# Attention in a hybrid encoder layer: the values product for four query blocks at once, with y_b parts, operand places and y_a low parts moved

## The chip, the cores and the metric

One core of a Trainium2 chip. TensorE (PE) multiplies and transposes into PSUM, VectorE (DVE), ScalarE (ACT) and GpSimd (POOL) do the elementwise work, SyncE (SP) issues most DMAs. The metric is the device time of one execution in microseconds.

## What is computed

One layer with sandwich norms, sequence 1024, width 1024, eight heads of 64, float32. Cut to what matters here:

```python
h = rms_norm(x, norm_mix_pre)
q, k, v, u, gates = split(h @ w_in)
# 64-row chunks; chunk c's queries see the keys of chunks c-8 .. c
y_a = chunk_band_attention(q, k, v, rel_bias) @ w_attn_out
y_b = multiscale_pool(u, w_pool_group, pool_scale) @ w_pool_out
g_a, g_b = split(sigmoid(gates + b_gate))
mix = (g_a * y_a + g_b * y_b) @ w_o
x = x + rms_norm(mix, norm_mix_post)
x = x + rms_norm(conv_gated_ffn(rms_norm(x, norm_ffn_pre), ...), norm_ffn_post)
```

## The kernel before

Each float32 operand is split into a high part (rounded to the matmul's type, by ACT) and a low part (the rest, a subtraction on DVE or POOL); a product is up to three matmuls: high x high, high x low, low x high. The helper `split` (L78) records both halves of a split and `mm3` (L84) the three products, so many instructions have these two lines: tiles tell them apart.

The stages in order: the input projection (tiles X_i, Y_i, Z_i), the attention with the y_b projection woven in, the y_a projection (tiles y), the product with w_o (tiles wops, L1117), and the feed-forward part (X_u, Y_u, Z_u and later X, Y, Z).

**Attention.** A head h has four steps J, each of two query blocks a of 128 rows. `scores(h, J)` multiplies queries and keys into `pst` (L850 for blocks with all 640 keys, L859 for the earlier, shorter ones); DVE adds the bias and takes the maximum (`sm`, L866), ACT takes the exponential (`pe`, L868), DVE the reciprocal (L870), POOL scales `pe` (L872). `transposed(J, pes)` turns `pe` block by block (L893, tiles `tp`, up to four in a PSUM bank); `split` copies each bank to `pth` (ACT) and `ptl` (DVE). There are two such pairs of buffers, for even and for odd J, each with six slots of 256 columns: a slot is a block of 128 keys, its columns are the two query blocks, and the corners that lie outside the band are zeroed once by POOL. `values_of(h, J)` multiplies the values `vv` with each slot, high and low, into `f` (L918): 256 columns at a time, 2, 4, 6 and 6 slots for J = 0 to 3. After every second J, ACT and DVE add the two halves of `f` (`sm2`, L926, L927) and split the sum into `ath` and `atl`, the left operand of y_a.

**y_b.** `yb_units` is a generator of 32 parts, six matmuls each (`ybp`, 128x512). The table `NU` says how many parts stand in each iteration i of the loop over the 32 (h, J) steps.

**Order.** Iteration i writes the scores of step i, the transposes of step i-1, y_b parts and the values of step i-2. A scheduler then sets the order of each engine's instructions from the written order and priorities; on the chip each engine runs its queue in that order and waits on semaphores.

**y_a.** Eight blocks m of 24 matmuls `y` (128x512, L84). `out_block` splits the weights `wr_ya`: the low part `wl_ya` on DVE for m = 0 and on POOL for the others. DVE then multiplies by the gate (L1036), adds y_b's part (L1037) and splits into `mix`. Two of the four pieces of w_o are split there too (`woh` on ACT, `wol` on POOL), the other two behind it on DVE. `y` has two PSUM buffers of two banks.

Of the kernel before, what the change touches and what calls it, by code (L numbers as in the profile page):

```python
# [17 lines left out]
P = 128  # L18
# [27 lines left out]
def trunk(ctx, tc, xn, xt, w_first, w_in, cols, gain_pre, bias, w_ao, w_pg, w_po, w_o, gains, w_up, w_dn, out):  # L46
# [25 lines left out]
    ident = const.tile([P, P], F32, name="ident")  # L72
# [293 lines left out]
    with ExitStack() as ph:  # L366
# [73 lines left out]
        A.activation(warm, warm, AF.Sqrt)  # L440
        make_identity(nc, ident)
# [338 lines left out]
    edge = ap_.tile([P, 8], F32, name="edge")  # L780
    G.memset(edge, 0.0)
# [28 lines left out]
    with ExitStack() as ph:  # L810
# [8 lines left out]
        psf.tile([P, 512], F32, tag="f", name="bankf")  # L819

# [17 lines left out]
        def scores(h, J):  # L838
# [3 lines left out]
            for a in range(2):  # L842
# [4 lines left out]
                if n == 640:  # L847
                    for c in range(2):
                        for x, kk in enumerate((kh, kl)):
                            last["pst"] = nc.tensor.matmul(  # L850
                                pst[:, 512 * c:512 * c + 320], qs[:, j * P:(j + 1) * P],
                                kk[:, k0 + 320 * c:k0 + 320 * c + 320],
                                start=x == 0, stop=x == 1)
                    sv = pst.rearrange("p (c n) -> p c n", c=2)[:, :, :320]
                    bv = bt.rearrange("p (c n) -> p c n", c=2)
# [8 lines left out]
                so = sm.rearrange("p (c n) -> p c n", c=2) if n == 640 else sm[:, :n]  # L864
# [11 lines left out]
        def transposed(J, pes):  # L876

            pth, ptl = PT[J % 2]
            fl = [t.rearrange("p s q -> p (s q)") for t in (pth, ptl)]
            (pa, na), (pb, nb) = pes  # L880
            sa, sb = 5 - na, 6 - nb
            if J == 0:
                banks = [[(pa, 0, 1, sa, 0), (pb, 0, 2, sb, 1)]]
            elif J == 1:
                banks = [[(pa, 0, 3, sa, 0)], [(pb, 0, 4, sb, 1)]]
            else:
                banks = [[(pa, 1, 4, 1, 0)], [(pa, 0, 1, 0, 0), (pb, 0, 1, 1, 1)], [(pb, 1, 4, 2, 1)]]
            for runs in banks:
                tp = psT.tile([P, 512], F32, tag="t", name="tp")
                c = 0  # L890
                for pe, b0, n, s0, a in runs:
                    for b in range(b0, b0 + n):
                        nc.tensor.transpose(tp[:, c * P:(c + 1) * P], pe[:, b * P:(b + 1) * P], ident)  # L893
                        c += 1
                if J >= 2 and len(runs) == 2:
                    moves = [(0, 2, [t[:, 0:768].rearrange("p (b q) -> p b q", b=2)[:, :, :P] for t in fl])]
                else:
                    moves, c = [], 0
                    for pe, b0, n, s0, a in runs:
                        moves.append((c, n, [t[:, s0:s0 + n, a * P:(a + 1) * P] for t in (pth, ptl)]))  # L900
                        c += n
                for c, n, (hi, lo) in moves:
# [659 lines left out]
```

## Time and profile before

| | |
|---|---|
| median of 3 runs | 1236.28 us (1236.08 to 1236.38) |
| the profiled execution | 1236.29 us; span 1234.5 us |
| PE, DVE, ACT, POOL busy | 1224.8, 949.9, 667.7, 211.5 us |
| attention with y_b | about 321.7 to 453.9 us |
| y_a | about 453.9 to 503.1 us |
| granted clock | 0.998 |

Times in the rows are microseconds from the start of the span, or ns where said. In a timeline row stand the start, the length, the engine, the line, the operation, out<-in, the shape and how many rows were merged; in brackets the engine's idle time before it and what ended that. In a row of windows stand the window, its length, each engine's busy time with the number of instructions, then the clock, the DMA share and GB/s. A matmul's length includes its passage through the array, which overlaps the next one's, so the distance between starts is what a matmul costs.

### The profile page before, as it was taken

Reading aid. Unit: us, or ns where it says so; the run is one execution under the profiler, and the core shown is the slowest. Engines: PE = TensorE matmul, PEld = TensorE weight load, DVE = VectorE, ACT = ScalarE, POOL = GpSimd, SP = SyncE. Lnnn points to the kernel's source line nnn. Section 1 sums busy time; section 2 is a strip of 40 time slices with the busy share of each in tenths; the row PEclk is TensorE's granted clock in tenths of the full one; section 3 lists DMA queues with packets and bytes.
Section 4 is the critical chain, followed back from the end, with each engine's and each line's share of the span. In section 5 each row is a group of like instructions: output and inputs, shape, how many; then the busy total and the mean of one; then the engine's idle time right before and its main releaser. Section 6 shows DMA issues by size and latency. Waiting matters only on the chain.

```text
span 1234.5 us, 16243 instructions
## 1 busy us (share of the span) xinstructions
PE 1224.8 (99%) x5743; PEld 1020.3 (83%) x5743; DVE 949.9 (77%) x1551; ACT 667.7 (54%) x1171; POOL 211.5 (17%) x184
## 2 busy tenths in 40 slices
PE   9999999999999999999999999999999999999997
PEld 7888888888889987888888888888888888888886
DVE  5898677866788878756799887667666675999968
ACT  6764355555577773434546555554545455445553
POOL 0000000043254545000000112433333300000000
PEclk9999999999999999999999999999999999999999
DMA  9879245438886845322352332122122117902103
GB/s 329 332 261 347 85 148 206 155 123 263 294 273 214 264 175 210 137 86 78 110 198 109 111 145 103 70 84 102 52 102 86 60 68 255 350 18 103 35 1 137
DMA packets 63857, 193.84 MB, mean 157 GB/s; under 512 B 6048, under 2 KB 6688, under 8 KB 58656
## 3 DMA queue, kind: packets, MB, share of 16 engines
q1 hardware_dynamic: 55712, 176.55, 40.6%
q10 hardware_dynamic: 7056, 12.59, 2.7%
q0 software_dynamic: 1008, 3.67, 0.7%
q8 instruction: 45, 0.74, 0.2%
q14 instruction: 36, 0.29, 0.1%
HBM read 139.84 MB, written 52.95 MB: 156 GB/s over the span
## 4 chain that ended last, share of the span: by engine, by line
PE 92%; DVE 6%; issue 1%; DMA 0%; ACT 0%; POOL 0%; DVEq 0%; SPq 0%; ACTq 0%
PE X_u L84 19%; PE X_i L84 12%; PE Y_u L84 10%; PE Y_i L84 9%; PE X L84 7%; PE wops L1117 7%; PE Z_u L84 4%; PE y L84 4%; PE Y L84 4%; PE ybp L84 3%; PE f L918 3%; PE tp L893 2%; PE Z_i L84 2%; PE first L466 2%; PE pst L850 1%; DVE a L1407 1%
## 5 line engine op out<-in xcount | busy, mean ns | idle before, releaser
L1241 DVE SCALAR_TENSOR_TENSOR hc<-hu,cv,hc 128x1022 f32<-128x1022 f32 (+1 forms) x88 | 115.5, 1315 | 27.8 <-ACT hc L1236 27.8
L78 ACT CAST wh_u<-s_u 128x512 fp32r<-128x512 f32 x88 | 54.5, 619 | 90.1 <-PE Y_u L84 47.7
L78 DVE TENSOR_TENSOR wl_u<-s_u,wh_u 128x512 fp32r<-128x512 f32 x88 | 62.4, 712 | 33.9 <-ACT wh_u L78 33.9
L78 ACT CAST wh_i<-s_i 128x512 fp32r<-128x512 f32 x64 | 39.9, 623 | 77.8 <-PE X_i L84 36.5
L78 ACT CAST wh_u<-wup 128x512 fp32r<-128x512 f32 x60 | 37.3, 622 | 51.7 <-PE X_u L84 27.5
L78 DVE TENSOR_TENSOR wl_i<-s_i,wh_i 128x512 fp32r<-128x512 f32 x64 | 46.5, 727 | 21.2 <-ACT wh_i L78 16.1
L1236 ACT ACTIVATE hc<-hu,cv 128x1024 f32<-128x1024 f32 x44 | 54.7, 1245 | 9.8 <-DVE hu L1185 8.9
L202 POOL TENSOR_TENSOR s_i<-win 128x512 f32<-128x512 f32 x4 | 5.9, 1480 | 257.0 <-DVE wl_i L78 246.5
L202 POOL TENSOR_TENSOR s_u<-wup 128x512 f32<-128x512 f32 x15 | 25.7, 1713 | 139.4 <-DVE wl_u L78 139.4
L78 DVE TENSOR_TENSOR ptl<-tp,pth 128x512 fp32r<-128x512 f32 (+3 forms) x80 | 42.9, 552 | 7.7 <-ACT pth L78 7.1
L868 ACT ACTIVATE pe<-sm,st 128x640 f32<-128x640 f32 (+2 forms) x64 | 44.4, 695 | 7.6 <-DVE st L866 7.5
L872 POOL TENSOR_SCALAR pe<-pe,st 128x640 f32<-128x640 f32 (+4 forms) x58 | 40.8, 708 | 43.5 <-DVE st L870 29.3
L78 ACT CAST pth<-tp 128x512 fp32r<-128x512 f32 (+3 forms) x80 | 36.4, 475 | 15.9 <-PE tp L893 11.0
L78 DVE TENSOR_TENSOR wl_u<-wup,wh_u 128x512 fp32r<-128x512 f32 x60 | 43.0, 719 | 1.2 <-ACT wh_u L78 0.5
L1246 ACT ACTIVATE hc<-hc 128x1024 f32<-128x1024 f32 x22 | 23.4, 1063 | 37.0 <-DVE hc L1241 36.9
L84 PE MATMUL ybp<-mx,wh_yb 128*128 128x512 f32 x128 | 43.3, 412 | 0.0
L866 DVE CUSTOM_DVE_ANT_0 sm<-pst,bt 128x640 f32<-128x640 f32 (+2 forms) x64 | 40.7, 652 | 2.9 <-issue 1.7
L206 POOL TENSOR_TENSOR s_u<-s_u,wup 128x512 f32<-128x512 f32 x15 | 19.4, 1292 | 102.2 <-DVE wl_u L78 99.6
L918 PE MATMUL f<-pth,vv 128*128 128x256 f32 x144 | 36.5, 286 | 0.0
L918 PE MATMUL f<-ptl,vv 128*128 128x256 f32 x144 | 36.5, 287 | 0.0
L208 POOL TENSOR_TENSOR s_u<-wup 128x512 f32<-128x512 f32 x15 | 32.2, 2143 | 23.5 <-DVE wl_u L78 23.5
L893 PE MATMUL tp<-ident,pe 128*128 128x128 f32 x240 | 35.4, 275 | 0.2
(524 smaller groups left out, 4136.2 us busy)
## 6 DMA issues: line engine op xcount, KB each, us to landing
wup<-in_w_up SPq DMA_DIRECT2D x22, 1024.0 KB, 5.0
win<-in_w_in SPq DMA_DIRECT2D x16, 1024.0 KB, 7.2
g_d<-hc SPq DMA_DIRECT2D x20, 512.0 KB, 2.6
sig_d<-d ACTq DMA_DIRECT2D x32, 256.0 KB, 2.1
a<-g_d SPq DMA_DIRECT2D x8, 1024.0 KB, 11.5
b<-in_w_dn SPq DMA_DIRECT2D x8, 1024.0 KB, 12.7
w<-in_w_in SPq DMA_DIRECT2D x12, 512.0 KB, 7.3
x<-in_xn SPq DMA_DIRECT2D x8, 512.0 KB, 8.9
```

What stands on the lines that cost most here:

```text
L78: return A.copy(hi, src), (eng or V).tensor_tensor(lo, src, hi.bitcast(F32), ALU.subtract)
L84: nc.tensor.matmul(ps, a[i], b[i], start=start and i == 0 and p == 0, stop=stop and i == n - 1 and p == 2, skip_group_check=True,)
L202: self.eng.tensor_tensor(self.s1, self.w21, self.w22, ALU.add)
L208: self.eng.tensor_tensor(self.s3, self.w11, self.w21, ALU.subtract)
L866: V.tensor_tensor_reduce(so, sv, bv, -1.0, 3e38, ALU.add, ALU.min, st[:, 0:1])
L868: A.activation(pe[:, :n], sm[:, :n], AF.Exp, scale=-1.0, bias=st[:, 0:1], accum_out=st[:, 1:2])
L872: (V if 4 * h + J in (0, 1, 31) else G).tensor_scalar(pe[:, :n], pe[:, :n], st[:, 2:3], 1.0, ALU.mult, ALU.mult)
L893: nc.tensor.transpose(tp[:, c * P:(c + 1) * P], pe[:, b * P:(b + 1) * P], ident)
L918: nc.tensor.matmul(fo, vv[:, kb, e].rearrange("p a d -> p (a d)"), t[:, s], start=s == slots[0] and x == 0, stop=s == slots[-1] and x == 1)
L1117: nc.tensor.matmul(ps[:, 512 * c:512 * c + 512], a[k // 4][:, k % 4, sl], wo[k][b][:, 512 * c:512 * c + 512], start=k == 0 and x == 0, sto ...
L1236: A.activation(c, hu, AF.Identity, scale=cv[:, C_CW + 88 + b:C_CW + 89 + b], bias=cv[:, C_CB + b:C_CB + b + 1])
L1241: V.scalar_tensor_tensor(c[:, n:], hu[:, :S - n], cv[:, w:w + 1], c[:, n:], ALU.mult, ALU.add)
```

## The change

1. Values. One pair of buffers of 20 blocks of 128 columns takes the place of the two pairs: five key blocks for each of four query blocks, so that the place of query block a and key offset d is 5a + d. `values_of` runs only after odd J, for four query blocks: for each key block one product over just the query blocks that see it, a strided operand of 1 to 4 blocks (128 to 512 columns). For J = 1 these are 4, 3, 2 and 1 blocks, for J = 3 they are 4, 4, 3, 3, 2, 2, 1 and 1; each high and low. No zeroed corners are left.
2. Order. In an iteration the y_b parts now stand right after the scores, then the values of the last pair, then the transposes. `NU` gives two parts in every even iteration from i = 4 and none in odd ones.
3. Scores of a 640-key block go as 384 + 256 columns in one row of `pst`, not as two of 320 in two banks.
4. Places. `edge` grows from 8 to 360 columns, `edge2` of 80 columns is new, and `ident` is made later. None is read but `ident`: they move what lies behind them. In the built programs the first bytes of the operands, modulo 512 bytes, are: ath 448 before and 64 now, pth/ptl 256 and 64, ident 480 and 64, pe 256 and 64; vv, wh_ya and the keys' high part are at 64 in both.
5. y_a. The low parts of all weights `wr_ya`, and of the two w_o pieces that are split in this stage, are made by DVE.

```diff
-    edge = ap_.tile([P, 8], F32, name="edge")
-    G.memset(edge, 0.0)
+    ap_.tile([P, 360], F32, name="edge")
...
+        atn.tile([P, 80], F32, name="edge2", bufs=1)
...
-                    for c in range(2):
+                    for c in (slice(0, 384), slice(384, 640)):
                         for x, kk in enumerate((kh, kl)):
                             last["pst"] = nc.tensor.matmul(
-                                pst[:, 512 * c:512 * c + 320], qs[:, j * P:(j + 1) * P],
-                                kk[:, k0 + 320 * c:k0 + 320 * c + 320],
+                                pst[:, P + c.start:P + c.stop], qs[:, j * P:(j + 1) * P],
+                                kk[:, k0 + c.start:k0 + c.stop],
                                 start=x == 0, stop=x == 1)
...
-                banks = [[(pa, 1, 4, 1, 0)], [(pa, 0, 1, 0, 0), (pb, 0, 1, 1, 1)], [(pb, 1, 4, 2, 1)]]
+                banks = [[(pa, 0, 4, k, 0)], [(pa, 4, 1, k, 4), (pb, 0, 1, k + 1, 0)], [(pb, 1, 4, k + 1, 1)]]
...
-            fo = f[:, 256 * (J % 2):256 * (J % 2) + 256]
-            for s in slots:
-                kb = 2 * J - 4 + s
-                for x, t in enumerate(PT[J % 2]):
-                    nc.tensor.matmul(fo, vv[:, kb, e].rearrange("p a d -> p (a d)"),
-                                     t[:, s], start=s == slots[0] and x == 0,
-                                     stop=s == slots[-1] and x == 1)
             if J % 2 == 0:
                 return
+            grid = [t.rearrange("p (a d) q -> p a d q", a=4) for t in PT]
+            slots = (4, 5, 6, 7) if J == 1 else (3, 4, 2, 5, 1, 6, 0, 7)
+            for s in slots:
+                kb = 2 * J - 6 + s
+                a0, a1 = max(0, s - 4), min(3, s)
+                for x, t in enumerate(grid):
+                    flat = t.rearrange("p a d q -> p (a d) q")
+                    at = 5 * a0 + s - a0
+                    nc.tensor.matmul(f[:, a0 * P:(a1 + 1) * P], vv[:, kb, e].rearrange("p a d -> p (a d)"),
+                                     flat[:, at:at + 4 * (a1 - a0) + 1:4],
+                                     start=s == slots[0] and x == 0, stop=s == slots[-1] and x == 1,
+                                     skip_group_check=True)
...
-        NU = [2, 2, 0, 1, 0, 1, 1, 2] + [0, 1, 1, 2] * 5 + [0, 1, 1, 1, 1, 1]
+        PT = [atn.tile([P, 20, P], F32R, name=f"pt{x}", bufs=1) for x in "hl"]
+        NU = [2, 2, 1, 1] + [2, 0, 2, 0] * 5 + [2, 0, 1, 0] + [1, 0, 1, 0, 1, 0]
...
+            with tc.issue_after(last["pst"].ins) if i < 2 else nullcontext():
+                for _ in range(NU[i]):
+                    next(units)
+            if i >= 2 and steps[i - 2][1] % 2:
+                values_of(*steps[i - 2])
             if 1 <= i <= len(steps):
                 transposed(steps[i - 1][1], pend.pop(i - 1))
...
-            out_block(wr, m, ath, atl, lambda s: y[:, s], "ya", G if m else V)
+            out_block(wr, m, ath, atl, lambda s: y[:, s], "ya", V)
...
-                split_wo(wraw[m // 2 - 1], wopa, G)
+                split_wo(wraw[m // 2 - 1], wopa)
```

What the scheduler makes of it is seen in the engines' queues. First PE in the middle of the attention, where a head's last transposes (J = 3) and the values that need them stand. Before:

```order
L859 MATMUL pst_3760<-qk3_3448 128x512
L859 MATMUL pst_3760<-kl3_3449,qk3_3448 128x512
L84 MATMUL ybp_3668<-mx09_2114,wh_yb3_3664 128x512
L893 MATMUL tp_3730<-ident_77,pe_3629 128x128 x4
L893 MATMUL tp_3770<-ident_77,pe_3704 128x128
L893 MATMUL tp_3770<-ident_77,pe_3714 128x128 x2
L84 MATMUL ybp_3668<-mx19_2115,wh_yb3_3664 128x512
L84 MATMUL ybp_3668<-mx09_2114,wl_yb3_3665 128x512
L84 MATMUL ybp_3668<-mx09_2114,wh_yb3_3664 128x512
L84 MATMUL ybp_3668<-mx19_2115,wh_yb3_3664 128x512
L84 MATMUL ybp_3668<-mx09_2114,wl_yb3_3665 128x512
L918 MATMUL f_3737<-pth1_3036,vv1_3214 128x256
```

The four transposes of bank tp_3730 are the last that the twelve products f_3737 need. Now, at the same place of a later head:

```order
L83 MATMUL ybp_4031<-mx05_1595,wh_yb5_4027 128x512
L916 MATMUL f_3973<-pth_3030,vv1_3207 128x512
L83 MATMUL ybp_4031<-mx15_1596,wh_yb5_4027 128x512
L891 MATMUL tp_3946<-ident_159,pe_3850 128x128 x4
L916 MATMUL f_3973<-ptl_3031,vv1_3207 128x512
L891 MATMUL tp_3995<-ident_159,pe_3901 128x128
L891 MATMUL tp_3995<-ident_159,pe_3911 128x128 x2
L850 MATMUL pst_4003<-qk4_3657 128x384
L916 MATMUL f_3973<-pth_3030,vv1_3207 128x512
L850 MATMUL pst_4003<-kl4_3658,qk4_3657 128x384
L850 MATMUL pst_4003<-qk4_3657 128x256
L850 MATMUL pst_4003<-kl4_3658,qk4_3657 128x256
```

The last transposes are now tp_3946; the third f (key block 4, high) needs them through ACT, the fourth, behind the score products that follow, through DVE. Five y_b products between transposes and values have become one f, three transposes and a score product.

PE again, where the values of J = 1 stand, now (before, they stood a step later, with y_b parts in between):

```order
L891 MATMUL tp_4051<-ident_159,pe_3969 128x128 x4
L850 MATMUL pst_4058<-qk4_3657 128x384
L850 MATMUL pst_4058<-kl4_3658,qk4_3657 128x384
L850 MATMUL pst_4058<-qk4_3657 128x256
L850 MATMUL pst_4058<-kl4_3658,qk4_3657 128x256
L850 MATMUL pst_4070<-qk4_3657 128x384
L850 MATMUL pst_4070<-kl4_3658,qk4_3657 128x384
L850 MATMUL pst_4070<-qk4_3657 128x256
L850 MATMUL pst_4070<-kl4_3658,qk4_3657 128x256
L916 MATMUL f_4082<-pth_3030,vv2_3665 128x512
L891 MATMUL tp_4096<-ident_159,pe_4011 128x128
L916 MATMUL f_4082<-ptl_3031,vv2_3665 128x512
```

Between the last transposes (tp_4051) and the first low product stand eight score products, one f and one transpose.

DVE in the y_a stage, blocks m = 2 and 3, before:

```order
L1036 TENSOR_TENSOR ya_4949<-y,ya_4949 128x1024
L1037 TENSOR_TENSOR ya_4949<-ya_4949 128x1024
L78 TENSOR_TENSOR mix00l<-ya_4949,mix00h 128x512
L78 TENSOR_TENSOR mix10l<-ya_4949,mix10h 128x512
L1036 TENSOR_TENSOR ya_4989<-y,ya_4989 128x1024
L1037 TENSOR_TENSOR ya_4989<-ya_4989 128x1024
L78 TENSOR_TENSOR mix00l<-ya_4989,mix00h 128x512
L78 TENSOR_TENSOR mix10l<-ya_4989,mix10h 128x512
```

and now:

```order
L1018 TENSOR_TENSOR ya_4843<-y,ya_4843 128x1024
L77 TENSOR_TENSOR wl_ya_5022<-wr_ya_4928,wh_ya_5021 128x512
L1019 TENSOR_TENSOR ya_4843<-ya_4843 128x1024
L77 TENSOR_TENSOR wol<-wo_4978,woh 128x1024
L77 TENSOR_TENSOR mix00l<-ya_4843,mix00h 128x512
L77 TENSOR_TENSOR mix10l<-ya_4843,mix10h 128x512
L1018 TENSOR_TENSOR ya_4883<-y,ya_4883 128x1024
L77 TENSOR_TENSOR wol<-wo_4978,woh 128x1024
L1019 TENSOR_TENSOR ya_4883<-ya_4883 128x1024
L77 TENSOR_TENSOR wl_ya_5072<-wr_ya_4976,wh_ya_5071 128x512
L77 TENSOR_TENSOR wl_ya_5107<-wr_ya_5018,wh_ya_5106 128x512
```

The low parts wl_ya and wol, which stood on POOL, are now between DVE's own instructions of the block.

More of the change, by code (lines that the diff above doesn't have):

```diff
@@ L440, in trunk @@
         A.activation(warm, warm, AF.Sqrt)
+        ident = const.tile([P, P], F32, name="ident")
         make_identity(nc, ident)
@@ L890, in transposed @@
                 c = 0
-                for pe, b0, n, s0, a in runs:
+                for pe, b0, n, a, d in runs:
                     for b in range(b0, b0 + n):
@@ L894, in transposed @@
                         c += 1
+                c = 0
                 if J >= 2 and len(runs) == 2:
[L896 to L902, printed above, removed]
-                    split(hi, lo, tp[:, c * P:(c + n) * P].rearrange("p (b q) -> p b q", b=n))
@@ L905, in trunk @@
[L905 removed]
+                    runs = [(None, 4, 2, k, 4)]
+                for pe, b0, n, a, d in runs:
+                    at = 5 * a + d
+                    split(PT[0][:, at:at + n], PT[1][:, at:at + n],
+                          tp[:, c * P:(c + n) * P].rearrange("p (b q) -> p b q", b=n))
+                    c += n
         def values_of(h, J):
             m, e = h // 2, h % 2
[L909 to L920 removed]
@@ L958, in trunk @@
         load_wy(2)
-        PT = []
-        for i in range(2):
-            pth = atn.tile([P, 6, 256], F32R, name=f"pth{i}", bufs=1)
-            ptl = atn.tile([P, 6, 256], F32R, name=f"ptl{i}", bufs=1)
-            for t in (pth, ptl):
-                G.memset(t[:, 0, 128:256].bitcast(F32), 0.0)
-                G.memset(t[:, 5, 0:128].bitcast(F32), 0.0)
-            PT.append((pth, ptl))
+        PT = [atn.tile([P, 20, P], F32R, name=f"pt{x}", bufs=1) for x in "hl"]
         units = yb_units()
-        NU = [2, 2, 0, 1, 0, 1, 1, 2] + [0, 1, 1, 2] * 5 + [0, 1, 1, 1, 1, 1]
+        NU = [2, 2, 1, 1] + [2, 0, 2, 0] * 5 + [2, 0, 1, 0] + [1, 0, 1, 0, 1, 0]
         steps = [(h, J) for h in range(H) for J in range(4)]
@@ L978, in trunk @@
                 pend[i] = scores(h, J)
-            if i == 1:
-                with tc.issue_after(last["pst"].ins):
-                    for _ in range(NU[i]):
-                        next(units)
+            with tc.issue_after(last["pst"].ins) if i < 2 else nullcontext():
[3 more added lines that the diff above has]
+                values_of(*steps[i - 2])
             if 1 <= i <= len(steps):
                 transposed(steps[i - 1][1], pend.pop(i - 1))
-            if i == 0:
-                with tc.issue_after(last["pst"].ins):
-                    for _ in range(NU[i]):
-                        next(units)
-            elif i > 1:
-                for _ in range(NU[i]):
-                    next(units, None)
-            if i >= 2:
-                values_of(*steps[i - 2])
         load_ya(0)
```

23 lines of the change are left out of this document (8 added, 15 removed).

## Prediction

> **What bounds the kernel now.** I read the page first, then the two stages the change touches as windows, then the rows of TensorE (PE) in time. The page says which engine sets the end:
>
> ```profile
> PE 1224.8 (99%) x5743; PEld 1020.3 (83%) x5743; DVE 949.9 (77%) x1551; ACT 667.7 (54%) x1171; POOL 211.5 (17%) x184
> ...
> PE 92%; DVE 6%; issue 1%; DMA 0%; ACT 0%; POOL 0%; DVEq 0%; SPq 0%; ACTq 0%
> ```
>
> PE is busy for 99% of the span and carries 92% of the chain that ended last. So I count the change in PE time, and then ask where PE will have to wait. By windows, the attention (first score product to first y product) and the y_a stage behind it:
>
> ```profile
> 321.70:453.90 132.20, 131.95 (x879) 118.50 (x879) 110.53 (x313) 99.22 (x244) 64.34 (x85) 1.00 0.70 232
> 453.90:503.10 49.20, 49.13 (x229) 39.77 (x228) 39.37 (x41) 20.25 (x33) 21.23 (x10) 1.00 0.59 211
> ```
>
> The columns are the length, then busy time of PE, weight loads, DVE, ACT and POOL. PE has no idle worth naming, at the full clock (1.00); DVE is busy 110.53 of 132.20 (84%), ACT 75%. A matmul's row lasts longer than its share, since they overlap, so prices are steps from start to start:
>
> ```profile
> 405.52 0.28 PE L918 MATMUL f<-ptl,vv 128*128 128x256 f32 x1
> ...
> 406.69 0.28 PE L918 MATMUL f<-ptl,vv 128*128 128x256 f32 x1
> 406.81 0.34 PE L859 MATMUL pst<-qk 128*128 128x384 f32 x1
> 406.99 0.33 PE L859 MATMUL pst<-kl,qk 128*128 128x384 f32 x1
> 407.16 0.39 PE L859 MATMUL pst<-qk 128*128 128x512 f32 x1
> 407.39 0.40 PE L859 MATMUL pst<-kl,qk 128*128 128x512 f32 x1
> 407.63 0.39 PE L84 MATMUL ybp<-mx,wh_yb 128*128 128x512 f32 x1
> ...
> 411.77 0.31 PE L850 MATMUL pst<-qk 128*128 128x320 f32 x1
> ...
> 412.36 0.92 PE L893 MATMUL tp<-ident,pe 128*128 128x128 f32 x7
> 413.04 0.49 PE L84 MATMUL ybp<-mx,wh_yb 128*128 128x512 f32 x1
> ```
>
> Ten steps of 256 columns take 1.17 us, so 0.117 us each; 384 columns 0.175; 512 columns 0.232 here; 320 columns 0.147 (four in 0.59). Seven transposes of 128 columns take 0.92, less 0.27 for the last one's own length: 0.109 a step. A transpose has half the columns of a 256-column product and costs nearly as much, so something other than its columns sets it.
>
> **The values product (f).** It had two groups of 144:
>
> ```profile
> L918 PE MATMUL f<-pth,vv 128*128 128x256 f32 x144 | 36.5, 286 | 0.0
> L918 PE MATMUL f<-ptl,vv 128*128 128x256 f32 x144 | 36.5, 287 | 0.0
> ```
>
> 288 x 0.117 = 33.7 us. By the code, a head now issues 24 products instead of 36: six each of 512, 384, 256 and 128 columns. For eight heads that is 48 x (0.232 + 0.175 + 0.117 + x), with x the step of a 128-column product of this type. No row shows x. From below: half of the 256-column step, 0.058. From above: a 512-column step, 0.232, as it cannot cost more than four times its columns. I take the transposes' 0.109, the only 128-column rows. Then f is 48 x 0.633 = 30.4, a gain of 3.3; at the ends a gain of 5.7 or a loss of 2.6.
>
> The row's reading has a rule beside it: the Trainium skill ("TensorE: Matmul & The Clock Gate", LDWEIGHTS) puts a weight load at its columns over 1.2 GHz, an estimate of 107 ns for 128, which agrees with 0.109 and would bound x too. Against it stands "FP8 and Floating Point Precision", TensorE Precision Notes: true FP32 takes four passes through the array; were the short products to run so, the sum would be that of the upper end. No run here shows which.
>
> **Scores.** A 640-key block goes as 384 + 256 instead of 320 + 320, twice: 0.584 against 0.590. Nothing. The copies out of tp are as many and as large as before, only contiguous: nothing. The nine memsets on POOL that fall away lay beside PE work: nothing.
>
> **New waits of f.** The two buffer pairs of probabilities become one, and f for four query blocks runs in one burst every second step, right behind the score products. Before its low half can be read, the last transposes must go through ACT and DVE:
>
> ```profile
> 457.06 0.66 PE L893 MATMUL tp<-ident,pe 128*128 128x128 f32 x4
> 457.81 0.59 ACT L78 CAST pth<-tp 128x512 fp32r<-128x512 f32 x1 [0.61 <-PE tp L893]
> 458.43 0.69 DVE L78 TENSOR_TENSOR ptl<-tp,pth 128x512 fp32r<-128x512 f32 x1 [1.09 <-ACT pth L78]
> 459.18 0.39 PE L918 MATMUL f<-ptl,vv 128*128 128x256 f32 x1
> ```
>
> From the last transpose's start (0.27 before 457.72) the high half is readable after 0.27 + 0.09 + 0.59 + 0.06 = 1.01 us, the low half after 0.27 + 1.46 = 1.73. What PE has in between, in the new order: at J=1 a transpose 0.11, eight score products 1.17, one f 0.23, one transpose 0.11, in all 1.62, so 0.11 short for the low half. At J=3 f 0.23, four transposes' rest 0.11, three transposes 0.33, one score product 0.175, in all 0.85, so 0.16 short for the high half; the low half then has 0.85 + 0.16 + 0.23 + 0.76 (five score products) = 2.0, enough. That is 0.27 a head with ACT and DVE free. Both queues are full most of the time, with the softmax of the next step behind this same copy, so I take 0.35: 2.8 for eight heads. Nothing can be gained here; the upper end is 0.3 more for each of 16 bursts, less than half of one score reduction standing ahead in DVE's queue:
>
> ```profile
> L866 DVE CUSTOM_DVE_ANT_0 sm<-pst,bt 128x640 f32<-128x640 f32 x32 | 25.8, 818 | 1.2 <-POOL pe L872 0.4 <-PE pst L850 0.3 <-issue 0.2
> ```
>
> In one respect the order also blocks less: the copy of the next J=0 writes into the buffer f still reads, but its place waits only for the third and seventh product of the burst, which run before ACT gets there.
>
> **y_b in other steps (NU).** The same 32 parts, two at a time. What they cover now:
>
> ```profile
> 332.41 0.31 PE L850 MATMUL pst<-qk 128*128 128x320 f32 x1
> 332.55 0.31 PE L850 MATMUL pst<-kl,qk 128*128 128x320 f32 x1
> 333.01 0.66 PE L893 MATMUL tp<-ident,pe 128*128 128x128 f32 x4
> ...
> 349.57 0.40 PE L84 MATMUL ybp<-mx,wl_yb 128*128 128x512 f32 x1
> 349.97 0.41 PE L893 MATMUL tp<-ident,pe 128*128 128x128 f32 x2
> ...
> 417.09 0.40 PE L84 MATMUL ybp<-mx,wl_yb 128*128 128x512 f32 x1
> ```
>
> The period of a head is (417.09 - 349.57)/4 = 16.88. In each, a ybp step before the transposes takes 0.40 instead of 0.23: 0.17 of waiting for the normalised probabilities, which come through POOL. Nine or ten ybp products (2.1 us) now stand between a pair of scores and those transposes: seven times 0.17 is 1.2 gained. At the start, six ybp products move ahead of transposes that wait 0.46 - 0.15 = 0.31: 0.3 gained. On SP a few loads of y_b gates and weights move up or down by a step of 4 us; no wait for them stands in the chain: nothing.
>
> **y_a.** Two things change there: the left operand ath/atl moves to the weights' place modulo 512 bytes (448 against 64 in the program before, both 64 now), and seven weight low parts and four of w_o move from POOL to DVE.
>
> ```profile
> 465.06:479.77 14.71, 14.71 (x65) 1.00 0.42 146
> 481.01:502.85 21.84, 21.84 (x95) 1.00 0.54 192
> 640.12:653.04 12.92, 12.92 (x58) 1.00 0.75 264
> ```
>
> The first two are windows of y products from one start to another, the third of the FFN's (63, 94 and 57 steps: rows that only reach in at an edge are counted too). The steps are 233.5, 232.3 and 226.7 ns. If the place is the cause, y gains 63 x 6.8 + 94 x 5.6 ns = 0.96 us. From below the gain is none: in the attention, ybp steps are 0.23 with both operands at 64 already, though in short runs. I take 0.9, since the FFN's steps come from long runs like y's.
>
> POOL and DVE disturb each other there:
>
> ```profile
> 463.52 5.77 POOL L78 TENSOR_TENSOR wol<-wo,woh 128x1024 fp32r<-128x1024 f32 x2 [4.89 <-ACT woh L78]
> 469.26 1.74 POOL L78 TENSOR_TENSOR wl_ya<-wr_ya,wh_ya 128x512 fp32r<-128x512 f32 x1
> ...
> 472.72 2.18 DVE L1037 TENSOR_TENSOR ya<-ya 128x1024 f32<-128x1024 f32 x1
> ...
> 480.59 1.23 DVE L1037 TENSOR_TENSOR ya<-ya 128x1024 f32<-128x1024 f32 x1
> ...
> 482.50 0.69 DVE L78 TENSOR_TENSOR mix00l<-ya,mix00h 128x512 fp32r<-128x512 f32 x1 [0.69 <-ACT mix00h L78]
> ...
> 479.34 1.21 DVE L1036 TENSOR_TENSOR ya<-y,ya 128x1024 f32<-128x1024 f32 x1
> ...
> 480.23 0.40 PE L84 MATMUL y<-ath,wl_ya 128*128 128x512 f32 x1
> 480.70 0.47 PE L84 MATMUL y<-ath,wh_ya 128*128 128x512 f32 x1
> ```
>
> Under POOL's work the same DVE add takes 2.18 instead of 1.23, and PE waits once for a y bank (480.23 to 480.70: 0.24 over a step). With POOL out, DVE has for each m 1.21 + 1.23 + 2 x 0.69 = 3.8, plus 0.69 for the weights, plus 4 x 1.2 for w_o over two m: at most 6.9 for m = 2 and 3, against 24 steps of 0.227 = 5.4 on PE. It falls some 2 us behind, within the one bank of slack, and has caught up by m = 7. Gain 0.24; on the other side wl_ya5, behind w_o on DVE, lands at about its use: 0.2 lost. Together 0.0, and y as a whole -0.9.
>
> **Sum.** -3.3 + 2.8 - 1.2 - 0.3 - 0.9 = -2.9. The profiled execution took 1236.29 us (span 1234.5), the median of the runs is 1236.28: 1233.4. From no change this measurement tells about 0.2%, 2.5 us.
>
> **Rivals.** A: short products of 128 columns are not bound by their weight load and cost like 512 (0.232). For it: no row of that width and type exists, and from 256 to 512 columns the step follows the columns, so the type's own bound is unseen. Against: transposes of that width run at 0.109. It adds 48 x 0.123 = 5.9: 1239.3, slower; it turns the sign from x = 0.17. B: each burst finds DVE or ACT busy, 0.3 more for 16: 1238.2. For it: DVE's 84%; against: its order puts the copies before the next reduction. C: the place modulo 512 does nothing: 1234.3; for it, the 0.23 of ybp. The Trainium skill ("SBUF — State Buffer", two separate sides) says PE never waits on another's port, which by that rule gives C. D: the short products cost their columns, 0.058: 1231.0.
>
> **How the numbers follow.** Main case 0.48 (its own range 1231.8 to 1235.0), A 0.20, B 0.15, C 0.10, D 0.07. Faster by over 0.2% (below 1233.8): main 0.32, D 0.07, C 0.05, B 0.02, so 0.46. Slower (above 1238.8): A 0.14, B 0.05, so 0.19. The rest, 0.35, is within. The range goes from 1230.4, below D, to 1239.3, A.
>
> **What would show it.** The f groups: steps of 128-column rows at 0.109 or 0.23. Idle of PE ahead of the third or fourth f of a J=3 burst, and the second of J=1, near 0.15. A head's period near 16.6. y steps at 226.7 without the pause at m = 3; DVE adds all 1.23. The forecast is wrong if x is above 0.17 or the bursts wait over 0.7 a head.

## The result: 2.5 us slower, where 2.9 us faster was forecast

| | before | after |
|---|---|---|
| median | 1236.28 us | 1238.78 us (1238.29 to 1239.03) |
| ratio, with its 95% interval | | 1.0019 (1.0013 to 1.0025) |
| span of the profiled execution | 1234.5 us | 1236.9 us |

The time lies within the range given (1230.4 to 1239.3), and on the other side of no change from the forecast. The page of after, busy times and the shares of the chain that ended last:

```profile
PE 1225.7 (99%) x5647; PEld 1013.3 (82%) x5647; DVE 953.3 (77%) x1562; ACT 669.0 (54%) x1171; POOL 189.1 (15%) x164
...
PE 89%; DVE 7%; ACT 2%; issue 1%; POOL 0%; DVEq 0%; ACTq 0%
```

PE has 96 instructions fewer and is "busy" 0.9 us longer; its share of the chain fell from 92% to 89%, and ACT has 2% of it. By windows, the attention and the y_a stage of after:

```profile
321.72:456.81 135.09, 132.81 (x788) 111.66 (x786) 112.20 (x312) 99.86 (x241) 61.28 (x74) 1.00 0.70 227
456.81:505.77 48.96, 48.74 (x223) 39.14 (x222) 41.12 (x52) 21.20 (x36) 1.30 (x1) 1.00 0.60 209
```

The attention went from 132.2 to 135.1 us, and PE, which had 0.25 us without a record there, now has 2.28. The y_a stage is 0.2 shorter, and what follows it 0.3. So the loss lies in the attention alone.

To see it by terms I took all starts of PE from the first score product to the first product with w_o. The work is the number of steps times their undisturbed length (512 columns 227 ns, 384: 175, 320: 147, 256: 117.5, a transpose 109, a 128-column f 94); by what a start came later than that is put to the instruction that started late: transposes (tp), values products (f), scores (pst), y_a (y) or y_b (ybp). The sums are net, since a start can also come early: behind the last transpose of a group the next instruction often starts after 0.03, not 0.109. In us:

| kernel | in all | work | late: tp | f | pst | y | ybp |
|---|---|---|---|---|---|---|---|
| before | 181.32 | 176.17 | 2.74 | 0.15 | 0.0 | 1.44 | 0.85 |
| after | 184.05 | 171.68 | 6.41 | 3.34 | 0.98 | 0.56 | 1.08 |

The work fell by 4.5, the lateness rose by 7.2: 3.7 at transposes, 3.2 at f, 1.0 at scores, 0.2 at ybp, and 0.9 less at y.

**Where transposes wait.** The first wait of a head in after, at the third bank of J = 2, with what ACT and DVE did ahead of it:

```profile
371.41 0.82 ACT L867 ACTIVATE pe<-sm,st 128x640 f32<-128x640 f32 x1
...
372.35 0.59 ACT L923 COPY sm<-f 64x512 f32<-64x512 f32 x1
...
372.95 0.86 ACT L77 CAST pth<-tp 128x512 fp32r<-128x512 f32 x2
372.96 0.68 DVE L924 TENSOR_TENSOR sm<-f,sm 64x512 f32<-64x512 f32 x1
...
373.58 1.02 DVE L77 TENSOR_TENSOR ptl<-tp,pth 128x512 fp32r<-128x512 f32 x2
...
373.85 0.39 PE L83 MATMUL ybp<-mx,wl_yb 128*128 128x512 f32 x1
...
374.42 0.63 PE L891 MATMUL tp<-ident,pe 128*128 128x128 f32 x4 [0.18 <-DVE ptl L77]
```

The ybp step of 0.57 instead of 0.23 is a wait of 0.34. It ends when DVE has copied the bank before the last (0.69 of the two copies from 373.58: 374.27; the transpose starts 0.15 later), not when POOL has scaled the probabilities: these were ready 6.0 us earlier. ACT's copy of f's half (0.59) and DVE's sum (0.68) stand ahead of the copies out of the bank. In heads 2 to 6 this wait is 0.34 to 0.45, and the second bank of J = 3 waits another 0.14 to 0.25, each time starting 0.06 us after the same kind of release. Over all heads of after, 16 groups of transposes start late and within 0.15 us of such a release, 4.4 us in all, and their probabilities had been ready for 2.0 us or more each time. In before the same count gives 9 groups and 1.5 us.

**What before had really waited for.** The rows ahead of the transposes at 349.97, which the prediction read as waiting for probabilities:

```profile
347.33 0.81 POOL L872 TENSOR_SCALAR pe<-pe,st 128x640 f32<-128x640 f32 x1 [0.29 <-DVE st L870]
...
348.11 1.29 POOL L78 TENSOR_TENSOR atl<-sm,ath 64x512 fp32r<-64x512 f32 x1
...
349.13 0.69 DVE L78 TENSOR_TENSOR ptl<-tp,pth 128x512 fp32r<-128x512 f32 x1
```

POOL had finished the scaling at 348.14, 1.83 us ahead. DVE's copy ends at 349.82, 0.15 before the transpose, as in after. The transposes have two PSUM banks; they waited for a bank already. In heads 3 to 8 it is the same, 0.15 after the copy and 0.6 to 0.8 after POOL. The wait of 0.31 at the start (333.01), though, was for probabilities: those transposes start 0.06 after POOL's scaling. In after both of these waits are gone, the one at the start and the one at the second bank of J = 2; the larger wait shown above stands one bank later.

**Bursts.** At J = 3 of after the third f waits for ACT's cast (378.67 + 0.59 = 379.26):

```profile
378.67 0.59 ACT L77 CAST pth<-tp 128x512 fp32r<-128x512 f32 x1 [1.31 <-PE tp L891]
...
379.31 0.50 PE L916 MATMUL f<-pth,vv 128*128 128x512 f32 x1
...
379.64 0.34 PE L850 MATMUL pst<-kl,qk 128*128 128x384 f32 x1
```

That f starts 0.24 late, measured by the step of the score product ahead of it, at 378.89 (0.16 if the transposes before that had all gone at 0.109). Its own step is 0.33 instead of 0.227: behind such a wait the next start comes 0.11 late too. What the 0.11 is no run shows. The Trainium skill ("TensorE: Matmul & The Clock Gate", LDWEIGHTS) puts a weight load at its columns over 1.2 GHz, an estimate of 107 ns for 128, which is near it. The profile's own rows of such a load last 0.19 and overlap the products.

**Short products** of the same head:

```profile
381.70 0.28 PE L916 MATMUL f<-ptl,vv 128*128 128x256 f32 x1
381.82 0.23 PE L916 MATMUL f<-pth,vv 128*128 128x128 f32 x1
381.88 0.27 PE L916 MATMUL f<-ptl,vv 128*128 128x128 f32 x1
381.99 0.27 PE L916 MATMUL f<-pth,vv 128*128 128x128 f32 x1
382.10 0.28 PE L916 MATMUL f<-ptl,vv 128*128 128x128 f32 x1
382.21 0.33 PE L850 MATMUL pst<-qk 128*128 128x256 f32 x1
```

The first step of a burst is 0.06, the others are 0.11 (0.094 on average over the 48, 4.54 us).

**y.** Two windows of y products of after, 60 and 95 steps:

```profile
466.10:479.70 13.60, 13.60 (x61) 11.03 (x61) 11.18 (x13) 8.43 (x12) 0.00 (x0) 1.00 0.46 165
481.05:502.60 21.55, 21.55 (x96) 17.83 (x95) 20.29 (x25) 7.58 (x13) 0.00 (x0) 1.00 0.62 213
```

And DVE's gate adds, in the view of the tile ya (count; shortest, median, longest in ns):

```profile
L1019 DVE TENSOR_TENSOR ya<-ya x7: 1212/1218/1226, 472.2 to 502.3; 128x1024 f32<-128x1024 f32 x7
```

Steps of 226.7 ns, no pause at m = 3, all adds at 1.21 to 1.23.

### The profile page after: what moved, and what is told of

Read it like the earlier page. It is cut to its first block, busy times and chain, and to the rows that moved or that the text cites. A ratio compares the mean times of both kernels' runs of the same rounds, so it can differ in the third digit from the quotient of the medians.

```text
span 1236.9 us, 16066 instructions
## 1 busy us (share of the span) xinstructions
PE 1225.7 (99%) x5647; PEld 1013.3 (82%) x5647; DVE 953.3 (77%) x1562; ACT 669.0 (54%) x1171; POOL 189.1 (15%) x164
## 4 chain that ended last, share of the span: by engine, by line
PE 89%; DVE 7%; ACT 2%; issue 1%; POOL 0%; DVEq 0%; ACTq 0%
PE X_u L83 19%; PE X_i L83 12%; PE Y_u L83 10%; PE Y_i L83 9%; PE X L83 7%; PE wops L1099 7%; PE Z_u L83 4%; PE Y L83 4%; PE y L83 3%; PE ybp L83 2%; PE Z_i L83 2%; PE first L466 2%; PE f L916 2%; PE tp L891 1%; DVE a L1389 1%; DVE b L1389 1%
## 5 line engine op out<-in xcount | busy, mean ns | idle before, releaser
L891 PEld LDWEIGHTS tp<-ident,pe 128*128 128x128 f32 x240 | 27.8, 140 | 11.5 <-issue 3.9
L83 PE MATMUL Y_u<-T1h,wl_u 128*128 128x512 f32 x88 | 34.2, 389 | 0.0
```

What stands on the lines that cost most here:

```text
L83: nc.tensor.matmul(ps, a[i], b[i], start=start and i == 0 and p == 0, stop=stop and i == n - 1 and p == 2, skip_group_check=True,)
```

## The experiments

The theory: the transposes wait for banks that DVE frees late, because of what the new order puts ahead of its copies. Rivals: they wait for scaled probabilities; the bursts make the loss; y_a or the places do.

### Parts 4 and 5 alone and together

```diff
+    ap_.tile([P, 360], F32, name="edge")              # and edge2, ident: e1
-            out_block(..., "ya", G if m else V)       # and split_wo: e2
+            out_block(..., "ya", V)
```

> The kernel before with part 4 alone (edge, edge2 and ident: all products of the attention and of y read both operands at place 64 modulo 512). If the place sets the y step (the prediction's term), the 192 y steps fall from 233 to 227 ns and the time by 0.9 to 1.1 us, to about 1235.3; the attention's period of a head stays 16.88. If the place does nothing (rival C), the time stays within 0.3 us and the y steps at 232 to 234 ns.

> The kernel before with part 5 alone (the low parts of wr_ya and of the two pieces of w_o on DVE instead of POOL). By the prediction's term the pause of 0.24 us at m = 3 goes, DVE's adds L1037 all take 1.23, and about 0.2 comes back at wl_ya5: no change, within 0.3 us. If DVE becomes the bound of this stage, its backlog of 2 us or more shows as waits of y products and the time is 1 to 2 us longer; if POOL's work slowed more than that pause, it is up to 0.7 us shorter.

> The kernel before with parts 4 and 5 together, the attention as it was. With the places alone the y steps fell from 232 to 227 ns, but the pause at m = 3 grew from 0.24 to 0.69 us and the f steps of 256 columns rose from 117 to 120 ns; with part 5 alone that pause was gone. Theory: the y gain of 1.0 becomes visible once POOL is out of y_a, on top of part 5's 1.0, less 0.6 for f: 1234.7 to 1235.3. Rival: the two do not add, and the time stays at that of part 5 alone, 1235.4, or at 1236.2. The difference to the changed kernel is then what parts 1 to 3 cost.

Measured: places alone 1236.21 (ratio 0.9999, 0.9990 to 1.0008); DVE alone 1235.36 (0.9992, 0.9983 to 1.0001); both 1234.48 (0.9986, 0.9978 to 0.9995). The places alone were expected at about 1235.3 and missed it, though the y steps are 227 (68 in the window below) with the queues of PE, DVE and ACT as in before: the pause at m = 3 took half of the gain, and f, whose 256-column steps rose from 117 to 120 ns (0.6 us), the rest. The window, and the rows of PE behind it:

```profile
464.50:479.94 15.44, 15.44 (x70) 12.77 (x68) 14.00 (x9) 6.03 (x10) 15.44 (x7) 1.00 0.44 161
```

```profile
480.17 0.39 PE L83 MATMUL y<-ath,wl_ya 128*128 128x512 f32 x1
481.08 0.47 PE L83 MATMUL y<-ath,wh_ya 128*128 128x512 f32 x1 [0.53 <-DVE ya L1036]
```

POOL is busy for all of that window, DVE's add comes later against a faster PE, and the wait is 0.69 instead of 0.24. DVE alone gained 0.9 where no change was expected, and mostly not at y: lateness there fell by 0.2, at transposes by 0.7 (2.74 to 2.04), in an order that the scheduler had changed. With both parts the lateness at y falls from 1.44 to 0.14 and at transposes to 1.98. So these two parts gain 1.8 us, and the first three cost 1238.78 - 1234.48 = 4.3.

### The place of f's operands

With the places the f steps of 256 columns rose; this run sets them back, with every queue the same as with parts 4 and 5.

```diff
-        atn.tile([P, 80], F32, name="edge2", bufs=1)
+        atn.tile([P, 128], F32, name="edge2", bufs=1)
```

> The kernel before with parts 4 and 5, but edge2 of 128 columns instead of 80: pth, ptl and pe lie at 256 modulo 512 again, as before, with vv at 64; ath stays at 64. Every engine's instructions and their order are the same as with 80. If the place sets the f step, it goes back from 120 to 117 ns, 288 x 2.5 ns = 0.7 us less: 1233.8. If the f step depended on something else, 1234.5 within 0.3 and 120 ns.

Ten f steps, first with the place at 64, then at 256:

```profile
405.74 0.28 PE L918 MATMUL f<-ptl,vv 128*128 128x256 f32 x1
...
406.93 0.28 PE L918 MATMUL f<-ptl,vv 128*128 128x256 f32 x1
```

```profile
405.69 0.28 PE L918 MATMUL f<-ptl,vv 128*128 128x256 f32 x1
...
406.82 0.28 PE L918 MATMUL f<-ptl,vv 128*128 128x256 f32 x1
```

1.19 against 1.13. Over all 288 f the steps sum to 36.44 and 35.79 us; the median step is 120 and 117 ns. So the steps went back as expected. Measured 1234.13 (0.9982, 0.9973 to 0.9991): the lowest median of all versions that keep every product, ahead of both kernels, though its interval overlaps that of 1234.48.

### Part 3 alone

```diff
-                    for c in range(2):
+                    for c in (slice(0, 384), slice(384, 640)):
```

> The kernel before with parts 3, 4 and 5: scores as 384 + 256 columns in one row of pst. By the steps (0.584 against 0.590 for a pair) the same as without part 3, 1234.5 within 0.4. If the uneven pieces or DVE's reduction over one row of 640 cost anything, the pst steps or the reductions' mean of 652 ns show it and it is 1 us or more longer.

Measured 1235.60 (0.9995, 0.9986 to 1.0003), more than the 1234.5 within 0.4 expected. The pst steps are as before; lateness grew by 0.7 at transposes and 0.5 at f, and the scheduler had put the queues in another order. Its interval overlaps that of 1234.48, so up to 1.1 us may be due to it.

### Part 2 alone: the order

```diff
-        NU = [2, 2, 0, 1, 0, 1, 1, 2] + [0, 1, 1, 2] * 5 + [0, 1, 1, 1, 1, 1]
+        NU = [2, 2, 1, 1] + [2, 0, 2, 0] * 5 + [2, 0, 1, 0] + [1, 0, 1, 0, 1, 0]
...                                     # y_b, then values, then transposes
```

> The kernel before with parts 4 and 5 (1234.5), and of the change's other parts only the order: NU with two parts in every second step, y_b ahead of the values and the values ahead of the transposes; the products of values stay at 256 columns, step by step, with two pairs of buffers. Theory: the order makes the waits of transposes (banks freed late in the half of a head in which twelve y_b products lie between scores and transposes), whatever the values' products are: some 0.8 a head at tp, 1238 to 1241. Rival: the order is harmless and the single pair with its bursts makes them: 1234 to 1236, and tp waits of 0.2 a head. By the prediction's term (the order gains 1.5): 1233.

Measured 1240.25 (1.0033, 1.0020 to 1.0045), 5.8 us above the same kernel in its old order, with the old products and both pairs of buffers. So the order costs by itself. The place was not as expected: lateness at transposes fell to 0.98, from 1.98, and at f it rose to 7.02. The transposes are covered better here; what the order uncovers is f. One of those waits:

```profile
393.89 0.60 ACT L77 CAST wh_ya<-wr_ya 128x512 fp32r<-128x512 f32 x1
...
394.40 1.07 ACT L77 CAST pth<-tp 128x512 fp32r<-128x512 f32 x2
...
395.03 0.38 PE L918 MATMUL f<-pth,vv 128*128 128x256 f32 x1 [0.28 <-ACT pth L77]
```

f now follows its transposes so closely that it waits for the same copies.

### The sum of f behind the transposes; one y_b part a step

```diff
-                values_of(*steps[i - 2])
+                fin = values_of(*steps[i - 2])        # products only
                 transposed(steps[i - 1][1], pend.pop(i - 1))
+                finish(*fin)                          # copy, sum, split
```

> The changed kernel, but the sum of f's halves and its split (ACT copy, DVE add, the cast to ath) are written behind the transposes of the same step, not ahead of them. Theory now: the transposes wait for a PSUM bank, since ACT's 0.59 and DVE's 0.68 for that sum stand ahead of the copies that free the bank. Then the wait after y_b (0.34 to 0.45 over a step, once a head) falls to 0.15 or less, the second one (0.14 to 0.25) too, and the time by 2 to 3.5 us, to about 1235.3 to 1236.8. Rival 1: they wait for the probabilities that POOL has scaled, as the prediction had it: then nothing moves (1238.8 within 0.5). Rival 2: the loss is in the bursts' own waits: the transposes' waits go, but PE waits as long at the f that follow: 1238.8.

> The changed kernel with the 32 y_b parts one in each step (NU 2, 2, 1, 1 and then 1 for 26 steps) instead of two in every second. Six y_b products now stand behind the score products of every step, so that J=1's burst has its low half in time (0.2 a head less with the weight load that follows a wait), and only six instead of twelve stand ahead of the transposes of even steps. By the theory (banks freed late) the transposes that stood behind twelve y_b products move closer to the sum of f and wait longer or as long: the time changes by less than 1 us either way, 1238 to 1239.8. By rival 1 (scaled probabilities late) those transposes lose 1.4 us of cover and wait for about that much more a head: 6 us or more slower.

> The changed kernel with one y_b part in each step, and the sum of f's halves behind the transposes. With one part a step, the wait that was left stood once in two heads, 0.73 to 0.94 us, at a transpose behind the sum of f (ACT 0.59, DVE 0.68). If that sum is what delays the bank, half or more of it goes: 8 heads, four waits, 1.5 to 2.5 us less than with one part a step alone, 1234.7 to 1235.7. If DVE's whole work in this half of a head is the limit, the wait only moves to the next transposes, as with two parts: 1237.2 within 0.4.

The sum moved behind the copies in both queues, and the time did not move: 1238.69 (1.0018, 1.0010 to 1.0027). Lateness at transposes fell from 6.41 to 4.92, at f it rose to 4.03 and at ybp to 2.17: 12.38 in all, against 12.37. In place of the old wait stands this one:

```profile
376.52 1.19 DVE L77 TENSOR_TENSOR wl_yb<-wr_yb,wh_yb 128x512 fp32r<-128x512 f32 x1
377.64 1.01 DVE L77 TENSOR_TENSOR ptl<-tp,pth 128x512 fp32r<-128x512 f32 x2
...
378.37 0.66 PE L891 MATMUL tp<-ident,pe 128*128 128x128 f32 x4
```

The next item in DVE's queue ahead of the copies, a y_b weight, now holds the bank. The expected 1235.3 to 1236.8 was missed; of the three, the second rival (the waits move) fits best. So the sum of f was what the wait showed, not what sets its size.

One part a step gave 1237.19 (1.0006, 0.9997 to 1.0015), below the 1238 to 1239.8 expected: less lateness at f (1.49), about as much at transposes (6.82), in single waits of 0.73 to 0.94 in every second head:

```profile
388.31 0.58 ACT L923 COPY sm<-f 64x512 f32<-64x512 f32 x1
...
388.92 0.69 DVE L924 TENSOR_TENSOR sm<-f,sm 64x512 f32<-64x512 f32 x1 [0.44 <-ACT sm L923]
...
389.65 1.02 DVE L77 TENSOR_TENSOR ptl<-tp,pth 128x512 fp32r<-128x512 f32 x2
...
390.40 0.44 PE L891 MATMUL tp<-ident,pe 128*128 128x128 f32 x2 [0.56 <-DVE ptl L77]
```

By the rival of scaled probabilities this should have lost 6 us; it gained 1.6. The combination missed its 1234.7 to 1235.7, but it came out of the scheduler in the same order as one part alone at these places, with the same waits, so it tells nothing more: 1237.99 (1.0014, 1.0005 to 1.0022).

### Three banks

```diff
-        psT = pool(ph, "psT", 2, space=PSUM)
+        psT = pool(ph, "psT", 3, space=PSUM)          # scores in one tile of 3 banks
```

> The changed kernel with three PSUM banks for the transposes instead of two; the bank comes from the scores, whose two blocks lie in one tile of three banks (each block has its own place, the middle bank is shared) instead of two tiles of two. If the transposes wait for banks, no transpose starts within 0.2 us of the release of the bank before the last any more, and of the 0.9 us a head that PE loses at transposes and at f, at least half goes: 3 us or more, to 1236 or less. If they wait for the scaled probabilities, or if DVE's and ACT's copies come too late for f whatever the banks, the waits move to f and the time stays at 1238.8 within 0.7. If the scores now wait for DVE's reduction of the step before, pst rows show it and the time is longer than 1239.

> The changed kernel with three banks for the transposes and the sum of f's halves behind them. If banks and that sum are the two causes, the waits left are those of the bursts for their copies (0.5 a head with the weight loads): 1235 or less, below three banks alone by up to 1. If DVE's load is the limit, it stays where three banks alone are, or where the changed kernel is, 1238.8.

Measured 1248.41 (1.0098, 1.0083 to 1.0113) and 1246.81 (1.0087, 1.0073 to 1.0100). The time decides nothing on banks: the scheduler made another order. In the first run the last y_b product stands at 457.7 us (after: 456.6) but the last values at 471.8 (after: 466.0, among y products), so 14 us of transposes and values had no cover, with waits up to 2.0 for scaled probabilities. The scores also waited for DVE's reductions, as the third expectation had it. The trace says a little more: in the first run only one group of transposes that starts on the release of its bank is late by over 0.1 (0.18), against 16 groups and 4.4 us in after. So in this other order the waits for banks went and others took their place; that a third bank would help the time stays open.

### A second pair of buffers

```diff
+        PT = [[... [P, 13, P] ...], [... [P, 20, P] ...]]   # J = 0 and 1; J = 2 and 3
-                pe = atn.tile(..., bufs=6)
+                pe = atn.tile(..., bufs=4)            # sm 3 -> 2, sm2 2 -> 1
```

With a second pair the values for four query blocks can stand in the order of before.

> The same second pair and the same smaller pe, sm and sm2, but with the order and NU of the change. It differs from the changed kernel by the pair and the buffers alone. If the order makes the waits, the time stays at 1238 to 1240. If the single pair of buffers does (copies that must stand behind the burst), it falls to 1233 to 1235.

> The changed kernel with the values for four query blocks, but a second pair of buffers for J = 0 and 1 (13 blocks), and with the order of before (transposes, then y_b parts, then values; NU of before); room comes from pe (four buffers, not six), sm (two, not three) and sm2 (one, not two). If the shorter values product is worth its 2.9 and the order made the waits, the time is 1234.5 - 2.9 = 1231.6, at most 1 more for the tighter buffers: 1231 to 1233. If bursts of four query blocks bring waits of their own whatever stands before them, it is 1234 to 1237. If the tighter buffers make reductions or exponentials wait, tp waits for pe show it and the time is above 1237.

> The kernel before with parts 4 and 5, and pe in four buffers (not six), sm in two (not three), sm2 in one (not two), as in the runs with a second pair. If these smaller buffers cost nothing, 1234.5 within 0.4. If they make exponentials or reductions wait, the transposes wait longer than 0.2 for probabilities and the time is 1236 or more; then part of what the runs with a second pair lost is theirs.

With the new order 1237.03 (1.0006, 0.9997 to 1.0015), between the two expectations: 1.7 us of the loss went with the single pair, though the interval still touches that of after. The smaller buffers alone gave 1235.17 (0.9991, 0.9982 to 1.0000), 0.7 above 1234.48 with overlapping intervals, so what the pair itself gives may be more. With the order of before it was 1241.37 (1.0042, 1.0029 to 1.0054), masked by a new wait of 0.9 to 1.6 us in each of the last six heads:

```profile
400.52 1.29 POOL L77 TENSOR_TENSOR atl<-sm,ath 64x512 fp32r<-64x512 f32 x1 [3.77 <-DVE st L869]
...
401.91 1.58 POOL L871 TENSOR_SCALAR pe<-pe,st 128x640 f32<-128x640 f32 x2
...
402.76 0.66 PE L892 MATMUL tp<-ident,pe 128*128 128x128 f32 x4 [1.02 <-POOL pe L871]
```

Here the probabilities are late: POOL scales them behind the low part of ath, and the transpose starts 0.06 after the first of the two. Three runs take that off POOL:

```diff
-            split(ath[r, m, qsl], atl[r, m, qsl], sm2[r], V if (h, J) == (7, 3) else G)
+            split(ath[r, m, qsl], atl[r, m, qsl], sm2[r], V)     # or V at J = 1 alone
```

> The second pair of buffers with the order of before, and the low part atl made by DVE at every step instead of by POOL. Theory: the 0.9 to 1.2 us that the transposes of J = 2 waited in every head stood behind atl (1.29 us) in POOL's queue; without it some 7 us go, and the waits left are those for banks (J0 0.15, J3c 0.2 to 0.3 a head): 1231 to 1234.5. Rival: DVE, with 0.7 us more twice a head, frees the banks later, and half or more of it comes back: 1236 to 1239.

> The same, but atl goes to DVE at J = 1 only, where it stood ahead of the probabilities of J = 2. If that place alone makes the wait, the J = 2 transposes wait 0.2 or less and the time is that of atl on DVE everywhere or up to 1 us less: 1231 to 1234.5. If POOL's queue is late for another reason, the wait at J = 2 stays at 0.9 to 1.2 and the time at 1240 to 1241.

> The second pair with the order of before, atl on DVE, and the scores of a 640-key block as 320 + 320 columns again. Part 3 alone had cost 1.1 us on the kernel before; if that is the pieces themselves, this is 1 us less than the same with 384 + 256; if it was only the order that came out of it, the two agree within 0.5 or differ either way.

At every step: 1235.99 (0.9997, 0.9988 to 1.0005), 5.4 us less and at the edge of what the rival expected; lateness at transposes fell from 11.28 to 4.38. At J = 1 alone: 1244.67 (1.0068, 1.0056 to 1.0081), against both expectations: the low part of J = 3, still on POOL, now stood between two scalings (384.17 us, for 1.26), and the transposes of the second block waited 1.6 to 2.0 in each of six heads; lateness at transposes 14.17. With 320 + 320 again: 1237.42 (1.0009, 1.0000 to 1.0018), slower and not faster than with 384 + 256, so the pieces themselves are not seen to cost anything; what part 3 costs depends on the order that the scheduler makes.

Thus even with a second pair, the old order and POOL relieved, 4.5 us less work came out 1.5 us slower than 1234.48. Up to 0.7 of that may be due to the smaller buffers, and DVE now makes atl as well.

### Does this stage pass on saved PE work?

```diff
                 for x, t in enumerate(PT[J % 2]):
+                    if x and (s == slots[0] or J == 3 and s == slots[1]):
+                        continue
```

> The kernel before with parts 4 and 5 (1234.5), leaving out 40 of the 144 low products of the values (that of the first key block of every step, and of the second at J = 3): 40 x 0.118 = 4.7 us less PE work, as much as the change saves, with the copies, the softmax and the written order as they were. If PE sets the pace of this stage and the bursts were to blame, the time falls by 4 us or more, to 1230.5 or less. If the chain through DVE, ACT and the PSUM banks sets it, PE waits instead and at most 2 us are gained: 1232.5 or more, with more excess in front of transposes and f.

Measured 1232.62 (0.9971, 0.9960 to 0.9982): 1.9 us less than 1234.48 for 4.7 us less work, just inside the second expectation. The attention, with all products and with 40 fewer:

```profile
321.70:453.86 132.16, 131.96 (x880) 119.37 (x878) 111.51 (x315) 99.14 (x244) 62.05 (x82) 1.00 0.70 232
```

```profile
321.60:451.93 130.33, 129.37 (x842) 115.12 (x841) 111.38 (x314) 99.41 (x243) 61.55 (x82) 1.00 0.69 235
```

DVE and ACT are busy as long as ever, PE has 0.96 without a record instead of 0.20. The lateness rose from 3.82 to 6.52: 1.4 at transposes, 0.7 at f. So about 0.4 of the saved PE work arrives here, and 0.6 turns into waits, without bursts and without the new order. (The scheduler ordered this program anew too, so the share is of this one run.)

The same account for the runs that carry the argument:

| kernel | in all | work | late: tp | f | pst | y | ybp |
|---|---|---|---|---|---|---|---|
| parts 4, 5 | 179.99 | 176.17 | 1.98 | 0.74 | 0.19 | 0.14 | 0.77 |
| and the order | 185.81 | 176.17 | 0.98 | 7.02 | 0.48 | 0.28 | 0.87 |
| and 40 f fewer | 177.99 | 171.47 | 3.37 | 1.48 | 0.37 | 0.28 | 1.02 |
| after, sum of f late | 184.07 | 171.68 | 4.92 | 4.03 | 0.87 | 0.39 | 2.17 |
| after, one part a step | 181.78 | 171.68 | 6.82 | 1.49 | 0.66 | 0.70 | 0.42 |
| two pairs, new order | 182.41 | 171.68 | 5.67 | 2.26 | 0.67 | 0.91 | 1.22 |
| two pairs, old order | 186.89 | 171.68 | 11.28 | 2.15 | 0.95 | 0.35 | 0.48 |
| and atl on DVE | 181.24 | 171.68 | 4.38 | 1.03 | 2.29 | 0.28 | 1.57 |

## Why the prediction was wrong

By its own terms, against the measured account:

| term | forecast | measured |
|---|---|---|
| f, with x = 0.109 | -3.3 | -4.4 (x = 0.094, 512 columns 0.227) |
| new waits of f | +2.8 | +3.2, and +1.0 at the scores behind them |
| y_b in other steps, start | -1.5 | +3.7 (all transposes) |
| y | -0.9 | -0.9 |
| scores, ybp | 0 | +0.1 |
| in all | -2.9 | +2.7 (and 0.3 less behind it) |

**The step that failed** is "y_b in other steps": that the 0.17 ahead of the transposes was "waiting for the normalised probabilities, which come through POOL", and that covering it with nine ybp products was a gain with nothing against it: the waits that the new order itself makes at transposes were put at nothing. It was a wait for a PSUM bank, and the trace of before said so (POOL done 1.83 us earlier, DVE's copy ending 0.15 before). The covered waits did go. But a bank is freed when ACT and DVE get to their copies, and the new order puts other work (the sum of f, y_b's gate and weights) ahead of those copies: the next bank waits 0.34 to 0.45, and one of J = 3 another 0.14 to 0.25. With all lateness at transposes put to it, the term has the wrong sign and is off by 5.2 us, nearly the whole error of 5.4. That puts waits down by the place where they appear. The order alone, with the old products, cost as much (5.8 us), but at f and not at transposes; so the term's sign is settled by a run of its own, while the split of the 4.3 us between the order, the single pair and part 3 is not.

**Behind it stands a second omission.** The sum counted every saved PE step at full value, since PE was busy 99%. In this stage only some 0.4 of 4.7 us saved arrived at the end, and moving the sum of f left the total of waits where it was. This suggests, without showing it, that the chain of softmax, copies and banks was nearly as long as PE's work; PE's 99% does not tell. A view of how long each bank was held, and by whom, is what the prediction lacked.

**What held.** The short products: x is on average below the transposes' step, and rival A (0.232) is out. The four passes that the Trainium skill ("FP8 and Floating Point Precision", TensorE Precision Notes) states for true FP32 do not show in these steps of 0.06 to 0.11. The bursts' waits are where they were looked for: 0.24 at the third f of J = 3 (0.16 was worked out), 0.10 at the second of J = 1, and 0.11 behind each, which the sum did not have. With the scores behind them that is some 0.5 a head against 0.35, below the 0.7 that was to refute it. The y steps are at 227, and the pause is gone. Against rival C: the place does something (232 to 227 ns for y, with the same queues on PE, DVE and ACT). The Trainium skill's rule ("SBUF — State Buffer", two separate sides), that PE never waits for another engine's port, says nothing of an operand's place, so C did not follow from it; no run here tests the rule itself. But the gain of the place needed part 5 to arrive, which the forecast, adding them, did not see, and part 5 alone measured 0.9 (its interval just includes none), not 0.0.

Rival B came nearest in time (1238.2), with a mechanism that is half right: the copies find DVE and ACT busy, but the transposes pay most of it, not the bursts (5.2 against 1.4 more than forecast). The head's period, forecast as 16.6, is 391.83 - 374.42 = 17.41:

```profile
391.83 0.63 PE L891 MATMUL tp<-ident,pe 128*128 128x128 f32 x4 [0.28 <-DVE ptl L77]
```

**Still open**: the price of a third bank, how the loss divides between the order and the single pair, and why the values for four query blocks with room and the old order are not ahead. The last run says that part of one saving was lost here, not which engine would have to be relieved.

## What to carry to other kernels

When a transpose or a product waits, list everything it needs (its operands, and the buffer it writes) with the end of each, and name the one that ended last; work laid over a wait that was put down to the wrong one may only move it: here it went at one bank and came back larger at the next. A PE that is busy 99% does not say that saved PE work arrives: take a few products out and time it before building a new scheme around the saving. Small gains that hide each other's waits, as places and POOL's work did here, are timed together as well as alone.

## What the hardware showed beyond the forecast

- Products of 128 columns went at 0.06 us for the first of a burst and at 0.11 for the others, 0.094 on average over 48.
- Behind an f that had waited for its copies, the next PE start came another 0.11 us late (0.33 instead of 0.227).
- The place of an operand modulo 512 bytes works both ways: with the weights at 64 in each case, y went from 232 to 227 ns as its operand moved from 448 to 64, and f (256 columns) from 117 to 120 ns as its operand moved from 256 to 64 and back to 117 with it. The same place for both is no rule.
- A transpose that waits for a bank starts 0.06 us after the end of the copy that frees it, or 0.15 where it also waits on a semaphore of a second engine (0.055 to 0.057 and 0.145 to 0.148 in these runs).
